# A two-layer decoder trunk: the pooling mixer pipelined, three background advances per pair, and weight low parts made by an adding transfer

## The chip, the cores and the metric

One core of a Trainium2 chip. The metric is the device time of one launch in microseconds, the median over runs. The program is issued in sequence on each engine: TensorE (PE) does matmuls, VectorE (DVE) and ScalarE (ACT) the work on rows, GpSimd (POOL) small things and, here, some transfers, SyncE (SP) issues the loads.

## The reference

Two layers over 1040 tokens (16 meta tokens and 1024 inputs) of width 1024, batch 1, float32:

```
for i in range(DEPTH):                      # 2
    a = rmsnorm(h, norm_mix_pre[i])
    if i % N_MIXERS == 0: m = mla_mixer(a, ...)           # layer 0
    else:                 m = pool_mixer(a, w_group, scale)  # layer 1
    h = h + rmsnorm(m, norm_mix_post[i])
    f = conv_ffn(rmsnorm(h, norm_ffn_pre[i]), w_up, conv_w, conv_b, w_down)
    h = h + rmsnorm(f, norm_ffn_post[i])
```

The pooling mixer works in four groups of 256 channels: the mean over the last 2, 4, 8 or 16 tokens less the token itself, times a 256 x 256 matrix of the group. The MLP has a width-3 causal convolution on both halves of its up-projection (2 x 2816 channels), then silu(gate) times value, then the down-projection.

## The kernel before

All dense work is done with channels on the 128 partitions and tokens along the free axis, in two halves: half 0 has 536 tokens, half 1 504. Every product of two float32 matrices is made of three matmuls per 128 x 128 block: high part by high part, high weight by low activation, low weight by high activation (`mm_half`). A weight tile comes from `wtile`: SP loads 128 x 1024 floats (512 KB) into `wr` (three buffers), ACT casts it to the high part `wh`, DVE subtracts to get the low part `wl` (four buffers each).

The MLP goes layer by layer, half by half, in two parts of 11 channel pairs. `ffn_up` makes for each pair a gate tile and a value tile: 24 matmuls of 506 columns in half 1, 48 of 260 to 268 in half 0 (two column cuts). ACT and DVE evict each into the convolution (`cv`), with a multiplication by `late` first in layer 0, half 0 (`u`). `ffn_down` then sums over the pairs. The PSUM pool has six one-bank buffers in half 1 and three two-bank buffers in half 0, handed out in program order.

Beside that runs the work of the other half, as a generator in the list `bg`: `after_ffn` reads the residual, does the norm behind the MLP (`post`), statistics (`inv_rms_steps`), the pooling mixer (`poolmix`), its norm and the norm ahead of the next MLP. `tick()` takes it one `yield` further, with a higher priority of its instructions in the scheduler; `ffn_up` does that twice per pair, `drain()` takes what is left at the end of a part. The scheduler of the framework then writes one order for each engine, and the engines keep to it. The statistics are a matmul with ones (`ps_st`, L82), a reciprocal root on DVE (`nv` ... `yh`, `yl`, L84 to L70), two diagonal matrices (`diag`, L115, one on DVE, one on POOL) and a matmul that spreads them over the partitions (`ps_bc`, L122).

`poolmix` shapes, for each group g and each of its two channel blocks, `pa` (normed input), g + 1 sums `psm`, `pmx`, and the split `xh` (ACT), `xl` (DVE); then come 24 matmuls of 268 columns in half 0 (12 of 504 in half 1) with the group's weights `pwh`, `pwl`, the eviction `F` on ACT and its sum of squares.

The stages that the text speaks of are named by layer and by the half whose up-projection runs: in "layer 0, half 1" the pooling mixer of half 0 is the background, in "layer 1, half 0" that of half 1.

Of the kernel before, what the change touches and what calls it, by code (L numbers as in the profile page):

```python
# [11 lines left out]
F32 = mybir.dt.float32  # L12
F32R = mybir.dt.float32r
I32 = mybir.dt.int32
ALU = mybir.AluOpType
# [31 lines left out]
class Kern:  # L47
# [553 lines left out]
    def dense(self):  # L601
        tc, nc, io, ctx = self.tc, self.nc, self.io, self.ctx
        P = lambda name, bufs, **kw: ctx.enter_context(tc.tile_pool(name=name, bufs=bufs, reuse_waits="tile", **kw))
        self.wp, self.ab, self.hp, self.gp = P("wp", 4), P("ab", 1), P("hp", 1), P("gp", 1)
        self.fp, self.up, self.tp = P("fp", 8), P("up", 2), P("tp", 5)
        stp = P("stf", 2, space=PSUM)
        self.stps = lambda name: stp.tile([128, 512], F32, tag="st", name=name)
        self.psum = None
        self.banks(1)
        self.dtile = lambda x: self.tp.tile([128, HALF], F32R, tag="x" + x, name="diag", bufs=2)  # L610
        self.H, self.A, self.bg = {}, {}, []

        F, acc = self.wo(0)
        self.bg.append(self.after_mixer(0, F, acc, 0, True))
        F, acc = self.wo(1)
        self.drain()
        self.bg.append(self.after_mixer(1, F, acc, 0, False))
        for L in range(2):
            self.L = L
            for hf in range(2):  # L620
                self.banks(2 - hf)
                Fa = None
                for part in range(2):
                    G = self.ffn_up(hf, part)
                    self.drain()
                    if part == 1 and hf == 0:
                        self.bg.append(self.pre(1, L))
                    if part == 1 and hf == 1 and L == 0:
                        self.bg.append(self.pre(0, 1))
                    if (L, hf, part) == (1, 1, 1):  # L630
                        self.ffn_down_last(part, G, Fa)
                        break
                    F, acc = self.ffn_down(part, G, Fa)
                    Fa = F
                    self.drain()
                else:
                    self.bg.append(self.after_ffn(hf, F, acc, L))
        self.drain()
# [13 lines left out]
    def after_mixer(self, hf, F, acc, L, pre):  # L652
        acc = yield from self.post(hf, F, acc, G_MIXPOST + 8 * L)
        if pre:

            self.late = yield from self.inv_rms_steps(acc, "xh", 2)
            yield from self.pre(hf, L, True)
        else:
            yield from self.ffn_norm(hf, acc)
# [41 lines left out]
        self.O[hf][0].append(hi)  # L701
        self.O[hf][1].append(lo)

    def wtile(self, src, nk, pool=False):
        nc = self.nc
        n = 128 * nk
        r = self.wp.tile([128, 1024], F32, tag="wr", name="wr", bufs=3)
        if pool:
            hi = self.wp.tile([128, 512], F32R, tag="pwh", name="pwh", bufs=1)
            lo = self.wp.tile([128, 512], F32R, tag="pwl", name="pwl", bufs=1)  # L710
        else:
            hi = self.wp.tile([128, 1024], F32R, tag="wh", name="wh")
            lo = self.wp.tile([128, 1024], F32R, tag="wl", name="wl")
        src = src if isinstance(src, list) else [src]
        for i, a in enumerate(src):
            w = n // len(src)
            nc.sync.dma_start(r[:, i * w:i * w + w], a)
        self.split(r[:, :n], hi[:, :n], lo[:, :n], lo_eng="dve")
        return [(hi[:, 128 * k:128 * k + 128], lo[:, 128 * k:128 * k + 128]) for k in range(nk)]

    @staticmethod
# [158 lines left out]
    def ffn_up(self, hf, part):  # L880
# [8 lines left out]
        for jj in range(JH):  # L889
            j = part * JH + jj  # L890
            cv = []
            for gv in range(2):
                idx = gv * NJ + j
                u, = self.mm_half(self.wtile(io["w_up"][L, j, :, gv], KD), ah, al, skip=skip)
                if (L, hf) == (0, 0):
                    t = self.up.tile([128, HALF], F32, tag="u", name="u")
                    nc.vector.tensor_tensor(t, u, self.late, op=ALU.mult)
                    u = t
                p0 = G_CONV + (L * 2 * NJ + idx) * 4
                c = self.tp.tile([128, HALF], F32, tag="t", name="cv")[:, :n]  # L900
                nc.scalar.activation(c, u[:, pad:pad + n], AF.Identity, bias=self.par(p0 + 3), scale=self.par(p0 + 2))  # L901
                for x in (1, 0):

                    o = max(0, 2 - x - pad)
                    nc.vector.scalar_tensor_tensor(c[:, o:], u[:, pad + x - 2 + o:pad + x - 2 + n], self.par(p0 + x),  # L905
                                                   c[:, o:], op0=ALU.mult, op1=ALU.add)
                cv.append(c)
                if gv == 0:
                    nc.scalar.activation(c, c, AF.Silu)  # L909
                    self.tick()  # L910
            nc.vector.tensor_tensor(cv[0], cv[0], cv[1], op=ALU.mult)  # L911
            hi = self.gp.tile([128, HALF], F32R, tag=f"gh{jj}", name="gh")[:, :n]
            lo = self.gp.tile([128, HALF], F32R, tag=f"gl{jj}", name="gl")[:, :n]
            self.split(cv[0], hi, lo, lo_eng="dve")
            gh.append(hi)
            gl.append(lo)
            self.tick()
# [57 lines left out]
    def poolmix(self, hf, R):  # L975
        nc, io = self.nc, self.io
        F, acc = [], None
        n_tok = HALVES[hf][1]
        end = n_tok + 16
        for g in range(4):  # L980
            win = 2 << g
            xh, xl = [], []
            for kk in range(2):
                k = 2 * g + kk
                a = self.tp.tile([128, HALF + 16], F32, tag="tc", name="pa")[:, :end]
                if hf == 0:
                    nc.gpsimd.memset(a[:, :16], 0.0)
                else:
                    nc.gpsimd.tensor_scalar(a[:, :16], self.phalo[:, k], 1.0, 0.0, op0=ALU.mult, op1=ALU.add)
                nc.vector.scalar_tensor_tensor(a[:, 16:], self.H[hf][k], self.par(G_MIXPRE + 8 + k), R,  # L990
                                               op0=ALU.mult, op1=ALU.mult)
                if hf == 0:
                    nc.gpsimd.tensor_scalar(self.phalo[:, k], a[:, n_tok:end], 1.0, 0.0,
                                            op0=ALU.mult, op1=ALU.add)
                s = a
                for l in range(g + 1):
                    d = 1 << l
                    lo, hi = 2 * d - 1, end
                    n = self.tp.tile([128, HALF + 16], F32, tag="tc", name="psm")[:, :end]
                    nc.vector.tensor_tensor(n[:, lo:hi], s[:, lo:hi], s[:, lo - d:hi - d], op=ALU.add)  # L1000
                    s = n
                mx = self.tp.tile([128, HALF + 16], F32, tag="tc", name="pmx")[:, :end]
                nc.vector.scalar_tensor_tensor(mx[:, 16:], s[:, 16:], 1.0 / win, a[:, 16:],
                                               op0=ALU.mult, op1=ALU.subtract)
                if hf == 0:
                    nc.vector.tensor_tensor(mx[:, 16:32], s[:, 16:32], self.par(G_CNT + 16 * g, 16), op=ALU.mult)
                    nc.vector.tensor_tensor(mx[:, 16:32], mx[:, 16:32], a[:, 16:32], op=ALU.subtract)
                hi_ = self.tp.tile([128, HALF], F32R, tag="xh", name="xh", bufs=2)[:, :n_tok]
                lo_ = self.tp.tile([128, HALF], F32R, tag="xl", name="xl", bufs=2)[:, :n_tok]
                self.split(mx[:, 16:], hi_, lo_, lo_eng="dve")  # L1010
                xh.append(hi_)
                xl.append(lo_)
                if kk == 0:
                    W = self.wtile(io["w_pool"][g], 4, True)
                yield
            for m in range(2):
                ps = self.mm_half([W[2 * kk + m] for kk in range(2)], xh, xl)
                f = self.fp.tile([128, HALF], F32, tag="F", name="F")[:, :n_tok]
                self.evac(f, ps, self.par(G_PS + 2 * g + m))
                F.append(f)  # L1020
                acc = self.addsq(acc, f)
            yield
        return F, acc


# [50 lines left out]
```

## Time and profile before

| | |
|---|---|
| median of 3 runs | 2246.76 us (2246.19 to 2248.37) |
| profiled run, its own time | 2246.28 us |
| its span | 2244.5 us |
| mean granted clock of PE | 0.984 of full speed |
| PE busy | 2154.0 us, 96% |
| DVE busy | 1459.2 us, 65% |
| ACT busy | 1046.9 us, 47% |
| POOL busy | 415.1 us, 18% |

The profiled run's time is 1.8 us longer than its span, which counts from the first instruction to the last. A row of the timeline gives the start, the length and the instruction, in brackets the idle time of its engine ahead of it and what ended that.

### The profile page before, as it was taken

The numbers are of one execution on the slowest core, as the hardware profiler recorded it, in microseconds if no ns is written. First come the engines' busy times: TensorE is split into PE (matmuls) and PEld (weight loads), VectorE is DVE, ScalarE is ACT, GpSimd is POOL, SyncE is SP. The second block draws the span as 40 slices with busy tenths as digits, with TensorE's granted clock in tenths as the row PEclk, the third lists the DMA queues.
The fourth block names the chain that finished last, engine by engine and source line by source line (L and its number), as shares of the span: only waits on it lengthen the run. The fifth ranks groups of instructions, "written<-read, shape, count | busy, mean of one in ns | idle before, by whom it ended". The sixth has DMA issues, their size and how long they took to land.

```text
span 2244.5 us, 36441 instructions
## 1 busy us (share of the span) xinstructions
PE 2154.0 (96%) x13968; PEld 1966.9 (88%) x13968; DVE 1459.2 (65%) x2686; ACT 1046.9 (47%) x1934; POOL 415.1 (18%) x755
## 2 busy tenths in 40 slices
PE   8889999998999999999998999999899999999996
PEld 8788888887989999999886888899899998888886
DVE  7877777776488725665887555587745557634655
ACT  6367777776454423433553344344433433433431
POOL 5677676764000000000000000000000000000001
PEclk9999999998999999999999999999999999999998
DMA  5011111114343232233223322422242245233321
GB/s 163 22 36 31 30 34 31 25 55 134 114 161 122 82 98 95 89 93 121 93 72 100 128 98 86 130 77 86 86 129 94 68 132 178 86 86 111 99 89 46
DMA packets 82902, 202.76 MB, mean 90 GB/s; under 512 B 10548, under 2 KB 31668, under 8 KB 82728
## 3 DMA queue, kind: packets, MB, share of 16 engines
q1 hardware_dynamic: 82584, 200.18, 28.5%
q8 instruction: 110, 1.80, 0.3%
q14 instruction: 64, 0.52, 0.1%
q10 hardware_dynamic: 144, 0.25, 0.0%
HBM read 179.15 MB, written 16.97 MB: 87 GB/s over the span
## 4 chain that ended last, share of the span: by engine, by line
PE 87%; DVE 5%; ACT 3%; issue 2%; POOL 2%; DMA 1%; SPq 0%; DVEq 0%; ACTq 0%; POOLq 0%
PE ps_m L758 72%; PE ps_t L579 2%; PE ps_s L528 2%; PE ps_o L564 1%; PE ps_o L565 1%; PE ps_s L530 1%; PE ps_s L529 1%; ACT P L542 1%; DVE ps_s L537 1%; PE ps_qk L409 1%; PE ps_st L82 1%; PE ps_qk L411 1%; PE ps_qk L410 1%; PE ps_bc L122 1%; DVE F L826 1%
## 5 line engine op out<-in xcount | busy, mean ns | idle before, releaser
L70 DVE TENSOR_TENSOR wl<-wr,wh 128x1024 fp32r<-128x1024 f32 (+3 forms) x316 | 349.4, 1106 | 420.2 <-ACT wh L64 411.8
L64 ACT CAST wh<-wr 128x1024 fp32r<-128x1024 f32 (+3 forms) x316 | 301.2, 953 | 591.9 <-PE ps_m L758 526.0
L758 PE MATMUL ps_m<-ah,wh 128*128 128x506 f32 (+2 forms) x2112 | 564.1, 321 | 3.4 <-ACT cv L901 1.7
L758 PE MATMUL ps_m<-al,wh 128*128 128x506 f32 (+2 forms) x2112 | 566.7, 322 | 0.0
L758 PE MATMUL ps_m<-ah,wl 128*128 128x506 f32 (+2 forms) x2112 | 563.3, 321 | 0.0
L758 PEld LDWEIGHTS ps_m<-ah,wh 128*128 128x128 f32 x2112 | 353.1, 189 | 34.9 <-ACT cv L901 1.9
L758 PEld LDWEIGHTS ps_m<-al,wh 128*128 128x128 f32 x2112 | 353.0, 189 | 28.3 <-issue 0.7
L758 PEld LDWEIGHTS ps_m<-ah,wl 128*128 128x128 f32 x2112 | 353.1, 189 | 27.8 <-issue 0.5
L758 PE MATMUL ps_m<-gh,wh 128*128 128x268 f32 (+3 forms) x1088 | 288.8, 318 | 1.9 <-ACT F L767 1.9
L758 PE MATMUL ps_m<-gh,wl 128*128 128x268 f32 (+3 forms) x1088 | 287.7, 317 | 0.0
L758 PE MATMUL ps_m<-gl,wh 128*128 128x268 f32 (+3 forms) x1088 | 287.4, 317 | 0.0
L905 DVE SCALAR_TENSOR_TENSOR cv<-ps_m,params,cv 128x504 f32<-128x504 f32 (+1 forms) x264 | 196.0, 744 | 3.2
L758 PEld LDWEIGHTS ps_m<-gh,wh 128*128 128x128 f32 x1088 | 182.9, 189 | 16.1 <-ACT F L767 2.1
L758 PEld LDWEIGHTS ps_m<-gh,wl 128*128 128x128 f32 x1088 | 181.9, 189 | 14.1 <-issue 0.5
L758 PEld LDWEIGHTS ps_m<-gl,wh 128*128 128x128 f32 x1088 | 182.2, 189 | 13.1
L115 POOL TENSOR_TENSOR diag<-ident,yl 65x260 fp32r<-65x260 f32 (+5 forms) x27 | 33.4, 1237 | 716.0 <-DVE yl L70 675.9
L64 ACT CAST gh<-cv 128x504 fp32r<-128x504 f32 (+2 forms) x88 | 54.7, 622 | 168.8 <-DVE cv L911 168.8
L542 ACT ACTIVATE P<-ps_s,stat 116x116 f32<-116x116 f32 (+9 forms) x160 | 111.5, 699 | 32.7 <-DVE stat L537 25.1
L579 PE MATMUL ps_t<-ident,P 116*116 116x116 f32 x720 | 113.2, 266 | 10.1 <-DVE ptl L593 5.4
L547 POOL TENSOR_SCALAR P<-P,stat 116x116 f32<-116x116 f32 (+2 forms) x144 | 109.3, 760 | 54.1 <-DVE stat L545 47.8
L909 ACT ACTIVATE cv<-cv 128x504 f32<-128x504 f32 (+2 forms) x88 | 55.8, 634 | 134.9 <-DVE cv L905 134.9
L579 PEld LDWEIGHTS ps_t<-ident,P 116*116 116x116 f32 x720 | 83.4, 136 | 23.3 <-DVE ptl L593 5.5
(199 smaller groups left out, 3600.1 us busy)
## 6 DMA issues: line engine op xcount, KB each, us to landing
wr<-in_w_up SPq DMA_DIRECT2D x176, 512.0 KB, 3.5
wr<-in_w_down SPq DMA_DIRECT2D x56, 384.0 KB, 3.1
wr<-in_w_down SPq DMA_DIRECT2D x56, 320.0 KB, 2.9
wr<-in_w_o SPq DMA_DIRECT2D x16, 512.0 KB, 3.8
resid<-H SPq DMA_DIRECT2D x16, 268.0 KB, 4.2
H<-resid SPq DMA_DIRECT2D x16, 268.0 KB, 3.4
xt<-in_x SPq DMA_DIRECT2D x32, 130.0 KB, 2.3
resid<-H SPq DMA_DIRECT2D x16, 252.0 KB, 3.7
```

The costliest lines, as they stand in the source:

```text
L64: nc.scalar.copy(hi, src)
L70: eng.tensor_tensor(lo, src, hi.bitcast(F32), op=ALU.subtract)
L82: nc.tensor.matmul(ps[:w, i:i + 1], acc[:, w * i:w * i + w], self.ones, start=True, stop=True)
L115: eng.tensor_tensor(t, self.ident[:w, :w].unsqueeze(1).broadcast_to([w, n, w]), part.bitcast(F32).unsqueeze(2).broadcast_to([w, n, w]), op ...
L122: nc.tensor.matmul(pb[:, :g * w], self.ones_r[:w], t[:, q:q + g].rearrange("p n w -> p (n w)"), start=i == 0, stop=i == 1)
L528: nc.tensor.matmul(ps[:n, x, :w], qh[:, qs], kh[:, ks], start=True, stop=False)
L542: nc.scalar.activation(dst, ps, AF.Exp, bias=mx[:n, 1:2], scale=-1.0, accum_out=es[:n, gi:gi + 1])
L547: nc.gpsimd.tensor_scalar(P[:n, :nk], P[:n, :nk], rs[:n], 1.0, op0=ALU.mult, op1=ALU.mult)
L579: nc.tensor.transpose(pt[:kn, x * QT:x * QT + n], Pi[:n, k0:k0 + kn], self.ident[:n, :n])
L758: nc.tensor.matmul(p, w, x[k][:, skip + c0:skip + c0 + m], start=k == 0 and w is wh and x is xh, stop=k == last and w is wl)
L905: nc.vector.scalar_tensor_tensor(c[:, o:], u[:, pad + x - 2 + o:pad + x - 2 + n], self.par(p0 + x), c[:, o:], op0=ALU.mult, op1=ALU.add)
L909: nc.scalar.activation(c, c, AF.Silu)
```

## The change

It has four parts. The up-projection's value tile is split into two runs of matmuls with a third `tick` between them, so a pair takes three advances in place of two. In `poolmix` the shaping of group g + 1 stands ahead of the matmuls of group g, and there are 9 yields in place of 12. In the first part of layer 0, half 1, and of layer 1, half 0 (44 weight tiles), the low part is no longer a subtraction on DVE: ACT writes the negative of the high part into `wl`, and a transfer of POOL's queue adds the 512 KB of `wr` onto it. Some temporaries get three buffers in place of two, and `u` shares the ring of `xl`.

```diff
-    def wtile(self, src, nk, pool=False):
+    def wtile(self, src, nk, pool=False, add=False):
...
-        self.split(r[:, :n], hi[:, :n], lo[:, :n], lo_eng="dve")
+        if add:
+
+            nc.scalar.copy(hi[:, :n], r[:, :n])
+            nc.scalar.activation(lo[:, :n], r[:, :n], AF.Copy, scale=-1.0)
+            nc.gpsimd.dma_start(lo[:, :n].bitcast(F32), r[:, :n], accum_op=ALU.add)
+        else:
+            self.split(r[:, :n], hi[:, :n], lo[:, :n], lo_eng="dve")
...
-                u, = self.mm_half(self.wtile(io["w_up"][L, j, :, gv], KD), ah, al, skip=skip)
+
+                W = self.wtile(io["w_up"][L, j, :, gv], KD, add=part == 0 and hf != L)
+                ps = self.mm_half(W[:KD // 2], ah, al, 0, KD, skip=skip, n=n + pad)
+                if gv == 1:
+                    self.tick()
+                u, = self.mm_half(W[KD // 2:], ah, al, KD // 2, KD, ps, skip, n + pad)
                 if (L, hf) == (0, 0):
-                    t = self.up.tile([128, HALF], F32, tag="u", name="u")
+                    t = self.tp.tile([128, HALF], F32, tag="xl", name="u", bufs=3)
...
+        X = [([], []) for _ in range(4)]
+        W = None
+        for g in range(5):
             for kk in range(2):
...
+                if g < 4:
+                    for dst, t in zip(X[g], shape(g, kk)):
+                        dst.append(t)
+                    yield
+                if g and kk == 0:
+                    for m in range(2):
+                        ps = self.mm_half([W[2 * x + m] for x in range(2)], *X[g - 1])
+                        f = self.fp.tile([128, HALF], F32, tag="F", name="F")[:, :n_tok]
+                        self.evac(f, ps, self.par(G_PS + 2 * (g - 1) + m))
+                        F.append(f)
+                        acc = self.addsq(acc, f)
+                if g < 4 and kk == 0:
                     W = self.wtile(io["w_pool"][g], 4, True)
-                yield
...
+        yield
         return F, acc
```

`shape` is the body of the old inner loop, unchanged but for three buffers of `xh` and `xl`. (`wl` is of the type fp32r, so the negative copy is rounded like `wh`, and the sum is again `wr` less `wh`.)

The order that results is shown at three places. First PE in layer 0, half 0, between two up-projection tiles (`ah`, `al` the activation, `wh`, `wl` the weights), at the second statistics of the other half. Before:

```order
L758 MATMUL ps_m<-ah,wh 128x268 x2
L758 MATMUL ps_m<-al,wh 128x268 x2
L82 MATMUL ps_st<-ones,acc 63x1 x8
L758 MATMUL ps_m<-ah,wl 128x268 x2
L758 MATMUL ps_m<-ah,wh 128x268 x2
```

The broadcast `ps_bc<-diag,ones_r` stood 74 rows behind this `ps_st`. Now the same engine has there:

```order
L764 MATMUL ps_m<-ah,wh 128x268 x2
L764 MATMUL ps_m<-al,wh 128x268 x2
L764 MATMUL ps_m<-ah,wl 128x268 x2
L82 MATMUL ps_st<-ones,acc 63x1 x8
L122 MATMUL ps_bc<-diag,ones_r 128x504 x2
L764 MATMUL ps_m<-ah,wh 128x268 x2
L764 MATMUL ps_m<-al,wh 128x268 x2
```

The broadcast has moved up to the ones matmul, with nothing between them.

Second PE in layer 0, half 1, at the end of the matmuls of group 2 of the pooling mixer and the first four of group 3 (`xh`, `xl` its input, `pwh`, `pwl` its weights). Before, with the down-projection's first tile (`gh`, `gl`) behind:

```order
L758 MATMUL ps_m<-xh,pwh 128x268 x4
L758 MATMUL ps_m<-xl,pwh 128x268 x2
L758 MATMUL ps_m<-xh,pwl 128x268 x2
L758 MATMUL ps_m<-xl,pwh 128x268 x2
L758 MATMUL ps_m<-xh,pwl 128x268 x2
L758 MATMUL ps_m<-xh,pwh 128x268 x4
L758 MATMUL ps_m<-gh,wh 128x504
```

Now the same rows stand between two tiles of the up-projection, with two more blocks of the first five rows ahead of them (the second half of group 1 and the first half of group 2):

```order
L764 MATMUL ps_m<-xh,pwh 128x268 x4
L764 MATMUL ps_m<-xl,pwh 128x268 x2
L764 MATMUL ps_m<-xh,pwl 128x268 x2
L764 MATMUL ps_m<-xl,pwh 128x268 x2
L764 MATMUL ps_m<-xh,pwl 128x268 x2
L764 MATMUL ps_m<-xh,pwh 128x268 x4
L764 MATMUL ps_m<-ah,wh 128x506
L764 MATMUL ps_m<-al,wh 128x506
```

So 12 + 24 + 4 pool matmuls have moved between two neighbouring tiles of the up-projection. DVE has, from the conv rows of the tile ahead (`cv_14627`) to the `pmx` that these last four need, 20 full-width instructions and 4 of 16 columns; the last twelve are:

```order
L1014 SCALAR_TENSOR_TENSOR pmx_14464<-psm_14462,pa_14454 128x536
L1001 SCALAR_TENSOR_TENSOR pa_14509<-H_13709,params_70,R_14110 128x536
L1017 TENSOR_TENSOR pmx_14464<-psm_14462,params_70 128x16
L1011 TENSOR_TENSOR psm_14513<-pa_14509 128x551
L1018 TENSOR_TENSOR pmx_14464<-pmx_14464,pa_14454 128x16
L1011 TENSOR_TENSOR psm_14515<-psm_14513 128x549
L70 TENSOR_TENSOR xl_14469<-pmx_14464,xh_14468 128x536
L1011 TENSOR_TENSOR psm_14517<-psm_14515 128x545
L1011 TENSOR_TENSOR psm_14519<-psm_14517 128x537
L1014 SCALAR_TENSOR_TENSOR pmx_14521<-psm_14519,pa_14509 128x536
L1017 TENSOR_TENSOR pmx_14521<-psm_14519,params_70 128x16
L1018 TENSOR_TENSOR pmx_14521<-pmx_14521,pa_14509 128x16
```

The shaping of group 3's first block (`pa_14509` to `pmx_14521`) has moved in among that of group 2, behind the conv of the tile ahead.

Third ACT in layer 1, half 0, ahead of the cast of group 3's first input. Before:

```order
L769 ACTIVATE F_18399<-ps_m_18392,params_70 128x504
L780 ACTIVATE sq_18389<-F_18387 128x504
L909 ACTIVATE cv_18375<-cv_18375 128x520
L780 ACTIVATE sq_18401<-F_18399 128x504
L64 CAST wh_18784<-wr_18783 128x640
L901 ACTIVATE cv_18459<-ps_m_18410,params_70 128x520
L64 CAST xh_18481<-pmx_18479 128x504
```

Now:

```order
L775 ACTIVATE F_17984<-ps_m_17977,params_70 128x504
L720 CAST wh_18301<-wr_18300 128x1024
L721 ACTIVATE wl_18302<-wr_18300 128x1024
L786 ACTIVATE sq_17974<-F_17972 128x504
L786 ACTIVATE sq_17986<-F_17984 128x504
L64 CAST xh_17929<-pmx_17927 128x504
```

A weight tile's cast and its new copy have moved between the eviction and the cast; the up-projection's own eviction (`cv_18459` before, `cv_18036` now) has moved ahead of these rows.

## Rows read from the trace of the kernel before

**Rows 1.** The page's first part: busy us, share of the span, instructions.

```profile
PE 2154.0 (96%) x13968; PEld 1966.9 (88%) x13968; DVE 1459.2 (65%) x2686; ACT 1046.9 (47%) x1934; POOL 415.1 (18%) x755
```

**Rows 2.** Waits of PE, 1000 to 1320 us: us in total, times, longest.

```profile
PE ps_m L758 <- ACT xh L64: 12.4, 2, 10.1
```

**Rows 3.** Waits of PE, 1420 to 1700 us.

```profile
PE ps_m L758 <- ACT xh L64: 2.7, 1, 2.7
PE ps_m L758 <- ACT F L767: 1.9, 1, 1.9
PE ps_m L758 <- ACT cv L901: 1.7, 1, 1.7
PE ps_m L758 <- DVE xl L70: 1.1, 1, 1.1
PE ps_m L758 <- ACT F L769: 0.3, 1, 0.3
```

**Rows 4.** Timeline of PE around the two waits of layer 0, half 1.

```profile
1169.72 1.06 PE L758 MATMUL ps_m<-xh,pwh 128*128 128x268 f32 x4 [2.30 <-ACT xh L64]
...
1173.72 0.40 PE L758 MATMUL ps_m<-ah,wl 128*128 128x506 f32 x1
1173.95 0.39 PE L758 MATMUL ps_m<-ah,wh 128*128 128x506 f32 x1
...
1190.18 1.26 PE L758 MATMUL ps_m<-xh,pwh 128*128 128x268 f32 x4 [10.12 <-ACT xh L64]
```

**Rows 5.** Windows: length, busy PE, PEld, DVE, ACT, POOL, granted clock, DMA share, GB/s.

```profile
1169.70:1173.50 3.80, 3.78 (x12) 3.19 (x13) 3.77 (x7) 0.63 (x1) 0.00 (x0) 0.55 0.35 108
1590.00:1600.00 10.00, 10.00 (x65) 9.51 (x64) 6.13 (x10) 4.25 (x7) 0.00 (x0) 0.84 0.06 8
```

**Rows 6.** Windows over layer 0, half 0 (first) and half 1, in up-projection.

```profile
673.30:729.40 56.10, 56.10 (x455) 55.17 (x454) 50.08 (x79) 25.89 (x36) 3.79 (x1) 1.00 0.37 122
1050.00:1177.40 127.40, 125.10 (x577) 104.15 (x578) 108.19 (x182) 61.60 (x94) 5.72 (x15) 0.99 0.27 85
```

**Rows 7.** Timeline of ACT and DVE ahead of the 10.12 us wait.

```profile
1178.03 0.77 ACT L901 ACTIVATE cv<-ps_m,params 128x504 f32<-128x504 f32 x1
1178.90 1.52 DVE L905 SCALAR_TENSOR_TENSOR cv<-ps_m,params,cv 128x504 f32<-128x504 f32 x2
...
1189.30 0.16 DVE L1007 TENSOR_TENSOR pmx<-pmx,pa 128x16 f32<-128x16 f32 x1
1189.49 0.64 ACT L64 CAST xh<-pmx 128x536 fp32r<-128x536 f32 x1 [6.29 <-DVE pmx L1007]
```

**Rows 8.** Timeline of statistics: POOL in layer 0, half 0, then a whole chain.

```profile
678.62 3.79 POOL L115 TENSOR_TENSOR diag<-ident,yl 63x504 fp32r<-63x504 f32 x1 [21.59 <-DVE yl L70]
...
1206.62 1.08 PE L82 MATMUL ps_st<-ones,acc 128*67 128x1 f32 x16
1208.32 0.15 DVE L84 TENSOR_SCALAR nv<-ps_st 67x8 f32<-67x8 f32 x1
...
1211.00 1.42 POOL L115 TENSOR_TENSOR diag<-ident,yl 67x536 fp32r<-67x536 f32 x1 [22.20 <-DVE yl L70]
```

**Rows 9.** Groups by shape: busy, mean ns of one, idle before and releasers.

```profile
L70 DVE TENSOR_TENSOR wl<-wr,wh 128x1024 fp32r<-128x1024 f32 x196 | 240.5, 1227 | 267.9 <-ACT wh L64 263.0 <-PE ps_m L758 2.3
L64 ACT CAST wh<-wr 128x1024 fp32r<-128x1024 f32 x196 | 206.1, 1051 | 334.8 <-PE ps_m L758 289.0 <-issue 40.2 <-DMA wr<-in_w_o 5.2
```

**Rows 10.** DMA issues: count, KB each, median us to landing.

```profile
wr<-in_w_up SPq DMA_DIRECT2D x176, 512.0 KB, 3.5
...
wr<-in_w_dqkv SPq DMA_DIRECT2D x6, 336.0 KB, 5.2
```

**Rows 11.** Timeline of POOL, two copies of 16 columns in layer 1, half 0.

```profile
1477.70 0.20 POOL L989 TENSOR_SCALAR pa<-phalo 128x16 f32<-128x16 f32 x1 [25.09 <-DVE acc L781]
1564.00 2.06 POOL L989 TENSOR_SCALAR pa<-phalo 128x16 f32<-128x16 f32 x1 [15.98 <-DVE psm L1000]
```

More of the change, by code (lines that the diff above doesn't have):

```diff
@@ L604, in dense @@
         self.wp, self.ab, self.hp, self.gp = P("wp", 4), P("ab", 1), P("hp", 1), P("gp", 1)
-        self.fp, self.up, self.tp = P("fp", 8), P("up", 2), P("tp", 5)
+        self.fp, self.tp = P("fp", 8), P("tp", 5)
         stp = P("stf", 2, space=PSUM)
@@ L609, in dense @@
         self.banks(1)
-        self.dtile = lambda x: self.tp.tile([128, HALF], F32R, tag="x" + x, name="diag", bufs=2)
+        self.dtile = lambda x: self.tp.tile([128, HALF], F32R, tag="x" + x, name="diag", bufs=3)
         self.H, self.A, self.bg = {}, {}, []
@@ L654, in after_mixer @@
         if pre:
-            self.late = yield from self.inv_rms_steps(acc, "xh", 2)
+            self.late = yield from self.inv_rms_steps(acc, "xh", 3)
             yield from self.pre(hf, L, True)
@@ L979, in poolmix, with shape @@
         end = n_tok + 16
-        for g in range(4):
+        def shape(g, kk):
             win = 2 << g
-            xh, xl = [], []
-            for kk in range(2):
[L984 to L1013, printed above, removed]
-                    W = self.wtile(io["w_pool"][g], 4, True)
-                yield
[L1016 to L1022, printed above, removed]
@@ new lines, in shape @@
+            k = 2 * g + kk
+            a = self.tp.tile([128, HALF + 16], F32, tag="tc", name="pa")[:, :end]
+            if hf == 0:
+                nc.gpsimd.memset(a[:, :16], 0.0)
+            else:
+                nc.gpsimd.tensor_scalar(a[:, :16], self.phalo[:, k], 1.0, 0.0, op0=ALU.mult, op1=ALU.add)
+            nc.vector.scalar_tensor_tensor(a[:, 16:], self.H[hf][k], self.par(G_MIXPRE + 8 + k), R,
+                                           op0=ALU.mult, op1=ALU.mult)
+            if hf == 0:
+                nc.gpsimd.tensor_scalar(self.phalo[:, k], a[:, n_tok:end], 1.0, 0.0,
+                                        op0=ALU.mult, op1=ALU.add)
@@ new lines, in shape @@
+            s = a
+            for l in range(g + 1):
+                d = 1 << l
+                lo, hi = 2 * d - 1, end
+                n = self.tp.tile([128, HALF + 16], F32, tag="tc", name="psm")[:, :end]
+                nc.vector.tensor_tensor(n[:, lo:hi], s[:, lo:hi], s[:, lo - d:hi - d], op=ALU.add)
+                s = n
+            mx = self.tp.tile([128, HALF + 16], F32, tag="tc", name="pmx")[:, :end]
+            nc.vector.scalar_tensor_tensor(mx[:, 16:], s[:, 16:], 1.0 / win, a[:, 16:],
+                                           op0=ALU.mult, op1=ALU.subtract)
@@ new lines, in shape @@
+            if hf == 0:
+                nc.vector.tensor_tensor(mx[:, 16:32], s[:, 16:32], self.par(G_CNT + 16 * g, 16), op=ALU.mult)
+                nc.vector.tensor_tensor(mx[:, 16:32], mx[:, 16:32], a[:, 16:32], op=ALU.subtract)
+            hi_ = self.tp.tile([128, HALF], F32R, tag="xh", name="xh", bufs=3)[:, :n_tok]
+            lo_ = self.tp.tile([128, HALF], F32R, tag="xl", name="xl", bufs=3)[:, :n_tok]
+            self.split(mx[:, 16:], hi_, lo_, lo_eng="dve")
+            return hi_, lo_
```

## The prediction, made before the changed kernel had run

> **What bounds the kernel now.** I read the page first, then the waits of TensorE (PE) in the two stages in which the pooling mixer runs as background work, then windows and the timeline around the waits found. The page shows PE busy 96% of the span, VectorE (DVE) 65%, ScalarE (ACT) 47%, GpSimd (POOL) 18% [rows 1]. PE's work is not changed by the edit: the order has as many matmuls after as before. So only PE's idle time can move, and it lies in few places. In layer 0, half 1, PE waits 12.4 us in two events, both for the cast `xh` of the pooling mixer on ACT [rows 2]; in layer 1, half 0, it waits five times, 7.7 us together [rows 3]. The timeline shows the two events: 2.30 and 10.12 us, each ahead of the four matmuls that read a first `xh` [rows 4].
>
> A wait costs more than its length. In the 3.80 us behind the 2.30 us wait the mean granted clock is 0.55, so it ran nearly all of it at the lower of the two levels (half of 2.4 GHz): 3.80 x 0.45 = 1.7 us lost. The stretch around the last wait of layer 1 stands at 0.84 over 10 us: 1.6 us lost [rows 5]. The bill of before is then 12.4 + 2 x 1.7 = 15.8 us in layer 0, half 1, and 7.7 + 1.6 = 9.3 us in layer 1, half 0. The stage of layer 0, half 0, has no bill: in its 56 us PE is busy all of the time [rows 6].
>
> Why PE waits: the second event's cast came when `pmx` was done, and DVE had worked without a gap since its conv rows at 1178.90: 15 full-width instructions and 2 narrow ones to 1189.46, so (10.56 - 0.33) / 15 = 0.68 us for a full-width one [rows 7]. DVE works its order in sequence. PE starves where the schedule puts pool matmuls closer behind a tile than DVE can shape their input.
>
> **The change part by part.**
>
> *Three advances per pair, layer 0, half 0.* Before, the ones matmul of the statistics (`ps_st`) and the broadcast (`ps_bc`) had 74 rows of up-projection between them; now nothing stands between (first place of the order above). PE has to sit through the whole chain: ones to `nv` 1208.32 - 1207.70 = 0.6 us, `nv` to the end of POOL's `diag` 1212.42 - 1208.32 = 4.1 us, 4.7 us together [rows 8]. POOL's `diag` of this very stage and shape took 3.79 us beside a busy DVE against 1.42 in that chain [rows 8], so the upper bound is 7.1 us. Below, some of it could be covered by matmuls still in flight: 4 us, with no loss of clock. I take 4.7 and a fall of the clock, 1.7, less 0.4 for matmuls in flight: **+6 us**. It is nearer the low end since the two DVE instructions that follow the chain there are few. What is late next are three evictions `u`, which stand behind `diag` on DVE; they start before POOL is done and are hidden by it. The same pair of rows in the other stages keeps a distance of 30 or more rows.
>
> *Pool matmuls of layer 0, half 1.* With three advances, two advances of one pair bring the matmuls of groups 1, 2 and the first four of group 3 between the same two tiles: 12 + 24 + 4 matmuls (second place of the order). At 0.123 us for 268 columns (56.10 / 455) [rows 6], the 36 ahead of group 3's are 4.4 us of work. DVE has, from the conv rows of the tile ahead to the `pmx` of group 3, 20 full-width instructions and 4 narrow: 20 x 0.68 + 4 x 0.17 = 14.3 us; an eviction on ACT ahead of them (0.8) and the cast behind (0.64) [rows 7] with some 0.2 between make 16.0. PE waits 16.0 - 4.4 = 11.6, and 1.7 of clock. The first group costs as well: its cast stands behind the tile's own eviction on ACT, and DVE has 9 full-width and 2 narrow instructions, 6.5 us, to do from the second last tile's end plus 1 us of eviction and 0.8 of cast, where a tile of 24 matmuls takes 24 x 0.23 = 5.5 us [rows 4]: 2.8 us, and 1.7. Four weight copies on ACT (4 x 1.05 [rows 9]) now stand ahead of group 2's second cast; up to 3 us of them could come on top, I take half. Sum 11.6 + 1.7 + 2.8 + 1.7 + 1.5 = 19.3 against 15.8: **+3.5 us** (bounds 0 and +8). The pipelined order doesn't remove this wait, it moves it from the start of the down-projection into the up-projection.
>
> *Layer 1, half 0.* Here ACT is late. Between the eviction `F` of group 2 and the cast `xh` of group 3 now stand a cast and the new copy of a weight tile, and two squares (third place of the order): 2 x 1.05 + 4 x 0.64 = 4.7 us with the eviction and the cast themselves [rows 7, 9], about 5 with latencies, and 1.6 of clock. The waits like those of before that stay, for evictions of the post step and first casts, I put at 3.9, half of the 7.7 of now [rows 3]. 5.0 + 1.6 + 3.9 = 10.5, and up to 1.5 where ACT waits for a load whose slot is still being added from, taken at half: 11.3 against 9.3: **+2 us** (bounds -2 and +6).
>
> *Fourth stage (layer 1, half 1).* Its background work has no statistics and no pool; 33 advances in place of 22 only bring it earlier. Nothing; the six PSUM buffers of that half cover it.
>
> *Low parts by adding transfers.* DVE loses 44 subtractions of 1.227 us, 54 us; ACT gains 44 copies like its casts of 1.05, 46 us [rows 9]. ACT was busy 61.6 of 127.4 us in the stage, DVE 108.2 [rows 6]: neither becomes the bound by its sum. PE lost 2.3 us in those 127 us, so the relief of DVE has almost nothing to win there. New is the transfer, X us long, between the copy and PE. It is hidden if a slot of `wr` turns round in three tiles, 3 x 5.5 = 16.5 us: load 3.5 [rows 10], two ACT passes 2.1, about 2 of queueing, which leaves X up to 8.9. The trace has no adding transfer. Bounds: below, the load of the same size, 3.5 us; above, the slowest load, 336 KB in 5.2 us, scaled to 512 KB: 7.9 [rows 10]. I take 7, twice the plain load, since the target is read too. It stays below 8.9, and the sum gets nothing from it. The Trainium skill (DMA: Bandwidth & Descriptors, section on the anatomy of a GpSimd-path DMA) gives 2.0 us plus bytes over 436 GB/s; for 512 KB that is an estimate of 3.2 us for a plain copy, by which the sum stays the same.
>
> Queued behind the adds on POOL stand the halo copies, memsets and `diag`, for which DVE, and for `diag` PE, waits. POOL idled 25 us ahead of one such copy [rows 11], which covers an add's wait of some us; without that cover each us is a us of PE.
>
> *Buffers.* `u`, `xh`, `xl` and the diagonals go from two to three buffers: less waiting or none, nothing counted. The same number of loads goes through SP, with W of a group one step later, behind its shape.
>
> *Sum.* 6 + 3.5 + 2 = +11.5 us on the profiled run's own 2246.28: 2257.8. That run lies 0.5 us below the median of the three, so I say **2258 us**.
>
> **The rivals.**
>
> *Faster: the pool waits vanish.* If DVE, 54 us lighter, runs ahead far enough that every first `xh` is there when PE comes to it, 15.8 + 9.3 are won and 6 lost: 2246.3 - 25.1 + 6 = 2227 us. For it speaks DVE's 85% in that stage (108.19 / 127.40) [rows 6]. Against it: the long row of shaping stands behind the conv of the tile ahead, which needs that tile's end, and the subtractions removed aren't in it. It decides where at most 6 of the 20 full-width rows are left when that tile ends. 12%.
>
> *The change does nothing that shows.* The long waits come out as before, and the statistics' gap is half covered: 2243 to 2250. For it: two of my three terms are differences of like numbers. 18%.
>
> *The add becomes the bound.* If X is above 8.9, the slot's ring is the clock: each us above it costs 1/3 us in each of 44 tiles, 15 us. X = 10 gives 2258 + 16 = 2274, X = 12 gives 2304. For it: a 16-column copy on POOL took 2.06 us in the midst of DVE work and 0.20 elsewhere [rows 11], so what POOL does for a transfer may take ten times as long while DVE runs, and DVE hardly pauses. Against it: 1.9 us more on 7 is at the limit, not over it. 12%. The Trainium skill (SBUF — State Buffer, section "Who interferes with whom") says that a DMA seen stalled by DVE is one issued from GpSimd, whose descriptors wait for a port pair that DVE holds; it infers that two-input DVE instructions spare the descriptors. The 2.06 us row agrees that POOL is held up; whether descriptors are, no row here shows.
>
> **How the numbers follow.** The forecast has 58%, on 2250 to 2270 by its bounds (+4, 0, -2 to +9, +8, +6, not all at one end). 2244 to 2276 leaves out the faster rival (12%) and the larger part of the slow add (8%). A measurement of this kernel tells 0.2%, 4.5 us, from no change. Faster 0.13, same 0.19, slower 0.68.
>
> **What would show it.** Right: a PE wait of 4 to 7 us at the broadcast in layer 0, half 0, for `diag`; one of about 11 us for ACT's `xh` of group 3 in layer 0, half 1, now ahead of an `ah` tile; one of about 5 us for `xh` in layer 1, half 0, with ACT busy; adds of 3.5 to 8 us and no PE waits for `wl`. Wrong: PE waits for `wl` in every tile (slow add), a broadcast without a gap, or group 3's `xh` ready when PE arrives.

## The result and the profile after

The changed kernel takes 2285.4 us (median of 5 runs, 2281.74 to 2289.98) against 2248.37 (2246.19 to 2248.99): 1.0172 times as long, 95% interval 1.0161 to 1.0182. The forecast was 2258, in 2244 to 2276. The direction was right, the size was not: 37 us slower in place of about 11. The profiled run took 2289.87 us. The first part of its page:

```profile
PE 2171.7 (95%) x13968; PEld 1982.4 (87%) x13968; DVE 1410.0 (62%) x2642; ACT 1086.9 (48%) x1978; POOL 454.1 (20%) x799
```

Beside [rows 1] PE has as many matmuls and is busy 17.7 us longer (its mean granted clock is 0.973 of full speed against 0.984), DVE lost 49 us, ACT gained 40. No engine but PE is near its limit. Where the time went shows in windows over the three stages that differ: layer 0, half 0; layer 0, half 1 with its first down-projection; layer 1, half 0 with its first down-projection. Columns as in [rows 5]; first the kernel before (two stages), then the changed one:

```profile
1042.70:1258.60 215.90, 203.48 (x971) 169.78 (x970) 166.71 (x290) 95.99 (x151) 9.49 (x20) 0.97 0.31 98
1440.20:1664.00 223.80, 216.11 (x1706) 209.04 (x1705) 160.21 (x265) 94.66 (x139) 10.30 (x12) 0.99 0.30 95
```

```profile
645.30:789.20 143.90, 139.73 (x1112) 137.57 (x1113) 111.30 (x188) 60.47 (x82) 4.12 (x3) 0.98 0.34 107
1050.10:1288.30 238.20, 209.56 (x971) 174.16 (x970) 145.46 (x271) 113.62 (x171) 30.05 (x39) 0.92 0.53 136
1470.80:1706.40 235.60, 222.05 (x1704) 214.50 (x1705) 138.62 (x245) 111.51 (x158) 25.09 (x31) 0.96 0.53 137
```

Layer 0, half 0 had 137.1 us up to its first down-projection (the same boundaries in the timeline, its first `ah` matmul to its first `gh`): +6.8. Layer 0, half 1: +22.3, of which PE's idle time is 16.2 (238.20 - 209.56 against 215.90 - 203.48) and 6.1 the clock (0.92 against 0.97). Layer 1, half 0: +11.8. That is 40.9 of the 43.6 us between the two spans. The waits of PE in the first, the second and the third stage, as in [rows 2] and [rows 3]:

```profile
PE ps_bc L122 <- DVE diag L115: 4.0, 1, 4.0
```

```profile
PE ps_m L764 <- ACT xh L64: 24.5, 4, 10.4
PE ps_bc L122 <- DVE diag L115: 3.9, 1, 3.9
```

```profile
PE ps_m L764 <- ACT xh L64: 8.6, 2, 7.7
PE ps_m L764 <- ACT F L775: 2.8, 1, 2.8
PE ps_st L82 <- DVE acc L787: 1.2, 1, 1.2
```

PE still waits for the first `xh` of a mixer group. But now ACT, which casts it, waits for something that the kernel before did not have in this stage. ACT's longest group of waits from 1050 to 1288 us:

```profile
ACT wh L720 <- DMA wr<-in_w_up: 30.9, 9, 6.3
```

ACT stands at the cast of a weight tile because its load has not come. The adding transfer is short: 5.1 us in the median, as the DMA issues show, beside the load's 3.6.

```profile
wr<-in_w_up SPq DMA_DIRECT2D x176, 512.0 KB, 3.6
wl<-wr POOLq DMA_DIRECT2D x44, 512.0 KB, 5.1
```

So look at when loads are issued. Timelines of PE at its longest wait, and of SP, POOL and ACT ahead of it:

```profile
1129.88 1.26 PE L764 MATMUL ps_m<-xh,pwh 128*128 128x268 f32 x4 [10.35 <-ACT xh L64]
```

```profile
1083.36 0.33 SPq L717 DMA_DIRECT2D wr<-in_w_pool  x1
1089.59 0.33 SPq L717 DMA_DIRECT2D wr<-in_w_up  x1
1090.01 0.38 SPq L717 DMA_DIRECT2D wr<-in_w_pool  x1
1097.90 0.33 SPq L717 DMA_DIRECT2D wr<-in_w_up  x1
1103.92 0.33 SPq L717 DMA_DIRECT2D wr<-in_w_pool  x1
1112.41 0.33 SPq L717 DMA_DIRECT2D wr<-in_w_up  x1
1122.92 0.33 SPq L717 DMA_DIRECT2D wr<-in_w_up  x1
```

```profile
1107.85 0.86 POOL L722 DMA_DIRECT2D wl<-wr  x1 [10.11 <-PE ps_m L764]
...
1118.31 0.87 POOL L722 DMA_DIRECT2D wl<-wr  x1 [5.04 <-ACT wl L721]
```

```profile
1116.00 1.05 ACT L720 CAST wh<-wr 128x1024 fp32r<-128x1024 f32 x1 [5.80 <-DMA wr<-in_w_up]
1116.95 1.06 ACT L721 ACTIVATE wl<-wr 128x1024 fp32r<-128x1024 f32 x1
1117.92 0.61 ACT L920 ACTIVATE cv<-cv 128x504 f32<-128x504 f32 x1
1118.43 0.76 ACT L912 ACTIVATE cv<-ps_m,params 128x504 f32<-128x504 f32 x1
```

Every second load is one of the mixer's weights (`in_w_pool`), in the same three buffers `wr`. Such a tile keeps its place until its cast `pwh` may be written, and that single buffer is free only when PE is done with the group before. The mixer's loads issued at 1090.01 and 1103.92 are cast only here:

```profile
1139.08 0.62 ACT L64 CAST pwh<-wr 128x512 fp32r<-128x512 f32 x1
1158.87 0.62 ACT L64 CAST pwh<-wr 128x512 fp32r<-128x512 f32 x1
```

So from 1103.92 to 1139 at least two of the three places are held, and the up-projection has one at most. Its loads come at 1112.41 and 1122.92, 10.5 us apart, one turn of that place: the add issued at 1107.85 lets the load go at 1112.41, the cast runs at 1116.00, the copy at 1116.95, the next add at 1118.31, the next load at 1122.92. A tile of matmuls lasts 5.5 us. Behind the cast, ACT has the conv evictions, which free PSUM and feed DVE, and the cast `xh` itself. So the load of 1122.92 leads straight to PE's longest wait: ACT waits for it, and the `xh` that PE needs at 1129.88 stands three instructions behind it.

```profile
1126.63 1.04 ACT L720 CAST wh<-wr 128x1024 fp32r<-128x1024 f32 x1 [3.98 <-DMA wr<-in_w_up]
...
1129.20 0.63 ACT L64 CAST xh<-pmx 128x536 fp32r<-128x536 f32 x1
```

### The profile page after: what moved, and what is told of

The parts are those of the page before. It is cut to its first block, busy times and chain, and to the rows that moved or that the text cites. A ratio compares the mean times of both kernels' runs of the same rounds, so it can differ in the third digit from the quotient of the medians.

```text
span 2288.1 us, 36519 instructions
## 1 busy us (share of the span) xinstructions
PE 2171.7 (95%) x13968; PEld 1982.4 (87%) x13968; DVE 1410.0 (62%) x2642; ACT 1086.9 (48%) x1978; POOL 454.1 (20%) x799
## 4 chain that ended last, share of the span: by engine, by line
PE 82%; DMA 5%; DVE 5%; ACT 4%; issue 2%; POOL 2%; SPq 0%; DVEq 0%; ACTq 0%; POOLq 0%
PE ps_m L764 69%; PE ps_t L579 2%; DMA wl<-wr 2%; PE ps_s L528 2%; DMA wr<-in_w_up 2%; PE ps_o L564 1%; PE ps_o L565 1%; PE ps_s L529 1%; PE ps_s L530 1%; ACT P L542 1%; DVE ps_s L537 1%; PE ps_qk L409 1%; PE ps_qk L410 1%; PE ps_qk L411 1%; PE ps_st L82 1%
## 5 line engine op out<-in xcount | busy, mean ns | idle before, releaser
L764 PE MATMUL ps_m<-ah,wh 128*128 128x506 f32 (+2 forms) x2112 | 570.7, 324 | 6.0 <-ACT F L775 2.8
L764 PE MATMUL ps_m<-al,wh 128*128 128x506 f32 (+2 forms) x2112 | 573.2, 325 | 0.0
L70 DVE TENSOR_TENSOR wl<-wr,wh 128x1024 fp32r<-128x1024 f32 (+3 forms) x272 | 294.8, 1084 | 416.8 <-ACT wh L64 413.6
L64 ACT CAST wh<-wr 128x1024 fp32r<-128x1024 f32 (+3 forms) x272 | 254.9, 937 | 508.4 <-PE ps_m L764 450.5
L764 PEld LDWEIGHTS ps_m<-ah,wh 128*128 128x128 f32 x2112 | 358.2, 192 | 39.1 <-issue 3.6
L764 PEld LDWEIGHTS ps_m<-al,wh 128*128 128x128 f32 x2112 | 358.0, 192 | 28.3 <-issue 0.7
L722 POOL DMA_DIRECT2D wl<-wr x44 | 38.3, 870 | 472.7 <-ACT wl L721 456.3
```

Source lines behind the costliest of these rows:

```text
L64: nc.scalar.copy(hi, src)
L70: eng.tensor_tensor(lo, src, hi.bitcast(F32), op=ALU.subtract)
L722: nc.gpsimd.dma_start(lo[:, :n].bitcast(F32), r[:, :n], accum_op=ALU.add)
L764: nc.tensor.matmul(p, w, x[k][:, skip + c0:skip + c0 + m], start=k == 0 and w is wh and x is xh, stop=k == last and w is wl)
```

## The experiments

Two theories stood against each other. The **ring theory**: the add makes a place of `wr` busy longer, and the mixer's weights take too many places, so loads are late. The **shaping theory**, which is the prediction's own: DVE's shaping stands too close behind a tile, and the add is innocent. All kernels are made from the changed one or from the one before. "Advances" are those per pair; "piped" is the pipelined mixer with the new buffers; the last word of a row says whose ring the mixer's weights load into. The stages' lengths (us) are from the timeline of each, from the first matmul of a stage to that of the next. Each ratio was measured beside runs of the kernel before on the same chip (medians 2247.15 to 2248.60).

| kernel | advances, mixer, low parts, mixer weights in | median us | ratio to before, 95% | L0 half 0 | L0 half 1 | L1 half 0 |
|---|---|---|---|---|---|---|
| before | 2, old, subtract, wr | 2248.37 | 1 | 137.1 | 215.9 | 223.8 |
| after | 3, piped, add, wr | 2285.4 | 1.0161 to 1.0182 | 143.9 | 238.2 | 235.6 |
| no_add | 3, piped, subtract, wr | 2270.49 | 1.0087 to 1.0117 | 142.8 | 230.7 | 226.5 |
| add_only | 2, old, add, wr | 2244.37 | 0.9976 to 0.9994 | 137.1 | 211.4 | 225.0 |
| own_ring_t4 | 3, piped, add, own | 2258.18 | 1.0036 to 1.0066 | 143.4 | 220.4 | 222.5 |
| two_ticks | 2, piped, add, wr | 2250.29 | 1.0001 to 1.0021 | 137.0 | 211.3 | 235.1 |
| t4_alone | 3, piped, add, wr | 2281.87 | 1.0134 to 1.0164 | 144.3 | 232.6 | 231.4 |
| own_ring_no_add | 3, piped, subtract, own | 2270.44 | 1.0081 to 1.0111 | 143.4 | 227.2 | 226.7 |
| third_only | 3, old, subtract, wr | 2279.07 | 1.0119 to 1.0153 | 137.1 | 241.5 | 229.9 |
| two_ticks_own_ring | 2, piped, add, own | 2230.13 | 0.9904 to 0.9935 | 137.0 | 199.5 | 223.4 |
| add_own_ring | 2, old, add, own | 2244.45 | 0.9979 to 0.9997 | 137.1 | 208.5 | 226.6 |
| two_ticks_own_no_add | 2, piped, subtract, own | 2245.32 | 0.9980 to 0.9999 | 137.0 | 209.4 | 224.4 |
| third_bufs | 3, old, subtract, wr, new buffers | 2284.28 | 1.0150 to 1.0180 | 143.0 | 240.4 | 229.3 |
| pipe_only | 2, piped, subtract, wr | 2241.11 | 0.9965 to 0.9983 | 137.0 | 208.5 | 224.4 |

**no_add**: the add undone.

```diff
-                W = self.wtile(io["w_up"][L, j, :, gv], KD, add=part == 0 and hf != L)
+                W = self.wtile(io["w_up"][L, j, :, gv], KD)
```

> The changed kernel with the subtraction on VectorE back; third advance, pipelined mixer and buffers stay. Ring theory (the three wr buffers turn round too slowly, because an add holds each some 6 us longer while the mixer's weights take every second place of the ring): layer 0, half 1 falls from 238 to about 219 us (up- and first down-projection), layer 1, half 0 from 236 to about 226, the kernel to about 2257; ScalarE's waits for wr loads under 1 us each. Shaping theory (the prediction's: VectorE's shaping of the mixer stands too close behind a tile, the add is innocent): VectorE gets 54 us more work, so both stages stay as long or get longer, 2285 or more. Both: the gap of 4 us at the broadcast in layer 0, half 0 stays.

Between the two: 15 us faster with 54 us more work on DVE, so the add is not innocent; but layer 0, half 1 is 230.7, not 219. A second cause is in it. Nor do ACT's waits for loads of the up-projection fall under 1 us each there: five are left, 10.2 us together.

**add_only**: the add on the kernel before, the same lines of `wtile` as in the change.

> The kernel before with the adding transfer alone, in the same 44 tiles; two advances and the mixer as before, whose weights take every fourth place of the ring. Ring theory: the add is dear only together with the denser mixer weights, so little shows here: 2247 to 2256. If the add's own delay between the load and the matmul is the cost, whatever the ring holds: 20 us or more, 2265 to 2280. Shaping theory: VectorE is relieved, 2240 to 2247.

Some 3.5 us faster than before. With the mixer's weights in every fourth place the add costs nothing and its relief shows, which is what the shaping theory had expected; the ring theory had put no gain here. The third guess, that the add's delay costs by itself, is out.

**own_ring_t4**: a buffer for the mixer's weights alone, the conv ring cut from five to four to make room.

```diff
-        r = self.wp.tile([128, 1024], F32, tag="wr", name="wr", bufs=3)
         if pool:
+            r = self.wp.tile([128, 512], F32, tag="pwr", name="pwr", bufs=1)
+        else:
+            r = self.wp.tile([128, 1024], F32, tag="wr", name="wr", bufs=3)
+        if pool:
...
-                c = self.tp.tile([128, HALF], F32, tag="t", name="cv")[:, :n]
+                c = self.tp.tile([128, HALF], F32, tag="t", name="cv", bufs=4)[:, :n]
```

> The changed kernel with a buffer of its own for the mixer's weight load (one, 512 columns), so wr serves the up-projection alone; the ring of the conv tiles cv is cut from 5 to 4 buffers to make room. Ring theory: an add may then take up to 8.9 us and takes 5.1, so ScalarE's waits for loads go and the kernel falls to about 2258 to 2265 (the prediction's own sum and its waits for shaping stay). Shaping theory: nothing changes but for the conv ring, 2283 to 2290.

2258.18, 27 us less. ACT's waits for loads in layer 0, half 1 fall from 30.9 us in nine to 3.7 in one, PE's from 28.7 to 14.7:

```profile
ACT wh L723 <- DMA wr<-in_w_up: 3.7, 1, 3.7
```

```profile
PE ps_m L767 <- ACT xh L64: 11.9, 3, 6.4
PE ps_m L767 <- ACT pwh L64: 2.8, 1, 2.8
```

**t4_alone**: its control, the second hunk above without the first.

> Control for the own ring: the changed kernel with the conv ring cv at 4 buffers and nothing else. If the 27 us that the own buffer won came from the wr ring: no gain here, 2280 to 2295. If the shorter conv ring did it (another order of the engines): 2255 to 2265.

2281.87: of the 27 us, some 24 are those of the place in `wr` (22 by the ratios), the rest is the conv ring's, no more than the spread of the runs.

**two_ticks**: the third advance undone, the split into two runs of matmuls kept.

```diff
-                if gv == 1:
-                    self.tick()
```

> The changed kernel without the third advance per pair; pipelined mixer, adding transfer and buffers stay. Both theories: the gap at the broadcast in layer 0, half 0 goes, 7 us. Ring theory: the mixer's weights take every third place or so, half of the ring's loss is left: 2262 to 2270. Shaping theory: the clusters of the mixer's matmuls are taken apart, both stages come back to their old length, 2245 to 2255.

2250.29, 35 us less. Layer 0, half 1 falls to 211.3, as the shaping theory said; layer 1, half 0 stays at 235.1, as it did not say. In this trace two of the up-projection's loads stand between two of the mixer's.

**own_ring_no_add**: own_ring_t4 with the edit of no_add.

> The own buffer for the mixer's weights (conv ring 4) with VectorE's subtraction back in place of the add; third advance and pipelined mixer stay. Ring theory: with wr for the up-projection alone the add costs nothing and its relief of VectorE is worth what it was on the kernel before, some 4 us: 2259 to 2266. If the add still delays weights there: faster than 2255.

2270.44, slower than expected by either: with three advances the relief by the add is worth 12 us, not 4. Beside no_add (2270.49) it shows that the own buffer, with the other order that it brings, is worth nothing without the add. Ring and add hurt together only.

**third_only**: the third advance put into the kernel before.

```diff
-                u, = self.mm_half(self.wtile(io["w_up"][L, j, :, gv], KD), ah, al, skip=skip)
+                W = self.wtile(io["w_up"][L, j, :, gv], KD)
+                ps = self.mm_half(W[:KD // 2], ah, al, 0, KD, skip=skip, n=n + pad)
+                if gv == 1:
+                    self.tick()
+                u, = self.mm_half(W[KD // 2:], ah, al, KD // 2, KD, ps, skip, n + pad)
```

> The kernel before with the third advance alone (the value tile's matmuls in two runs, a tick between); old mixer, VectorE's subtraction, old buffers. Mixer weights take every third place of the ring here. Ring theory: without the add a place is free some 6 us sooner, so waits for wr loads stay small; 7 us for the broadcast in layer 0, half 0, and shaping waits like those of before: 2252 to 2260. Shaping theory: three advances cluster the mixer by themselves and that is most of the change's cost: 2265 to 2285.

2279.07, as the shaping theory had it: three advances alone cost 30 us. PE waits 6.6 us for `diag` at the broadcast of layer 0, half 1, ahead of the mixer. The waits over the mixer's stretch there (from the first `pa` on DVE to its last matmul, 1109.31 to 1192.23) show the rest:

```profile
PE ps_m L758 <- ACT xh L64: 25.1, 4, 7.5
DVE acc L781 <- ACT sq L780: 12.0, 2, 6.1
DVE pwl L70 <- ACT pwh L64: 7.7, 1, 7.7
...
ACT F L769 <- PE ps_m L758: 21.2, 4, 6.3
ACT xh L64 <- DVE pmx L1011: 15.2, 7, 4.1
```

PE waits for ACT, ACT for DVE and for PE, DVE for ACT. No engine is full: the group goes round in sequence, shaping, cast, matmuls, eviction `F`, square, sum `acc`, and the next group's shaping stands behind that sum in DVE's order. Windows over the same stretch, of the kernel before, of third_only and of two_ticks_own_ring (below):

```profile
1116.61:1199.21 82.60, 70.18 (x335) 59.36 (x334) 67.85 (x110) 38.14 (x64) 3.55 (x15) 0.92 0.21 64
```

```profile
1109.31:1192.23 82.92, 58.33 (x260) 49.14 (x261) 55.20 (x92) 29.02 (x49) 2.75 (x15) 0.82 0.17 53
```

```profile
1104.91:1186.59 81.68, 81.68 (x402) 69.38 (x401) 65.90 (x112) 49.54 (x77) 14.77 (x24) 1.00 0.61 147
```

The mixer takes 82 to 83 us in all three. What changes is how much of the up-projection the schedule has put beside it: 335 matmul records, 260, 402. In this stage the third advance takes three tiles of cover away from the old mixer, and the mixer does not get shorter for it. That its length stays is not general, though. With the pipelined mixer the third advance does shorten the stretch, as the windows of pipe_only (two advances, below) and no_add (three) show:

```profile
1114.42:1189.82 75.40, 69.72 (x336) 58.86 (x335) 66.15 (x110) 36.59 (x61) 5.93 (x15) 0.95 0.24 76
```

```profile
1116.41:1177.36 60.95, 43.25 (x196) 36.73 (x197) 49.54 (x84) 24.56 (x43) 9.34 (x15) 0.75 0.19 61
```

The stretch loses 14 us, but the matmuls beside it fall from 336 to 196, and PE's idle time (length less busy time) grows by 12 us in both pairs: 12.4 to 24.6 in the old mixer, 5.7 to 17.7 in the pipelined one. The clock adds to it, 0.95 to 0.75. In layer 1, half 0, the old mixer's stretch falls from 95.9 to 72.2 us and PE's idle time in it still grows, from 4.1 to 9.1.

**two_ticks_own_ring**: the edits of two_ticks and own_ring_t4 together.

> Two advances, pipelined mixer, adding transfer, own buffer for the mixer's weights (conv ring 4). Ring theory: with two advances layer 1, half 0 still took 235 us, with mixer weights in every third place; with the own buffer it falls to 222 to 225, layer 0, half 1 stays at 209 to 212: 2236 to 2241, faster than the kernel before. Shaping theory: the stage of layer 1 is long by its shaping, so it stays: 2248 to 2252.

2230.13, faster than both kernels (0.9904 to 0.9935 of before) and than expected. Layer 0, half 1 has no PE wait left; its window:

```profile
1044.10:1243.60 199.50, 199.50 (x970) 167.11 (x969) 143.63 (x262) 112.73 (x170) 29.54 (x39) 1.00 0.63 160
```

**add_own_ring**: add_only with the edit of own_ring_t4.

> The kernel before with the adding transfer and the own buffer for the mixer's weights (conv ring 4); two advances, old mixer. If pipelining the mixer is a part of what made the best kernel so far (2230): the old mixer's long wait for group 3 stays, 2240 to 2246. If the add and the free ring do it alone: 2227 to 2233.

2244.45: the old mixer's wait for group 3 stays (6.84 us in the timeline). The pipelining is a needed part of 2230.

**two_ticks_own_no_add**: two_ticks_own_ring with the edit of no_add.

> The best kernel so far (two advances, pipelined mixer, own buffer) with VectorE's subtraction back in place of the add. If VectorE's load in the mixer's stretch is what sets the waits, its 54 us come back as waits in part: 2238 to 2246. If with two advances the pipelining alone removes the waits: 2228 to 2233.

2245.32: so is the add, worth 15 us there. (Against pipe_only, 2241.11, below, the own buffer without the add is 4 us slower.)

**third_bufs**: third_only with the new buffers (three of `xh`, `xl` and `diag`, `u` in the ring of `xl`).

> The kernel before with the third advance and the changed buffers (three of xh, xl and diag, u in the ring of xl); old mixer, subtraction. The third advance alone left layer 0, half 0 at 137 us, so if the buffers together with it bring broadcast and ones matmul together, the 4 us gap appears and the stage takes 143 to 144 us. If the pipelined mixer is needed for it: 137. The kernel: 2270 to 2288 in either case, less where the third buffer of xh and xl helps the mixer.

The gap at the broadcast appears in layer 0, half 0, 143.0 us against 137.1 in third_only. The waits of PE there:

```profile
PE ps_bc L122 <- DVE diag L115: 4.0, 1, 4.0
```

It needs the third advance and the buffers, not the pipelined mixer; two_ticks, with the buffers and two advances, has none.

**pipe_only**: the changed kernel with the edits of two_ticks and no_add.

> Pipelined mixer and changed buffers alone: two advances, subtraction, mixer weights in the ring of wr. Load theory (VectorE's work per pair sets the waits, the ring is harmless without the add): the long waits for group 2 and 3 of the old mixer spread and shrink, 2238 to 2247. Shaping theory as predicted (pipelining only moves the waits): 2245 to 2252. If dense mixer weights hurt without the add too: 2255 or more.

2241.11, 6 us faster than before in its own comparison: with two advances the pipelined mixer takes the 12.4 us of waits of layer 0, half 1 down to 5.7.

With these runs five pairs differ by the third advance alone: before to third_only (+30 us), pipe_only to no_add (+29), two_ticks to the changed kernel (+35), two_ticks_own_ring to own_ring_t4 (+28), two_ticks_own_no_add to own_ring_no_add (+25). Whatever stands beside it, it is the largest single cost of the change.

## Why the prediction was right and wrong

**Two steps failed.** In the prediction's own terms the miss splits in two. Everything but the add is no_add: 2270.49, +22 us where the sum had +11.5. The add on top costs 15 more, where the sum had nothing.

**The add** was priced at nothing by the step "It is hidden if a slot of `wr` turns round in three tiles, 3 x 5.5 = 16.5 us". The add's own time was in its bounds (5.1 us measured, 7 taken, 8.9 allowed). But the ring's three places do not serve three tiles. The prediction said that W of a group goes through SP "one step later" and did not ask whose place it takes: the mixer's weights stand in the same ring, in every fourth place before, in every second or third after, and each waits there for the group ahead, so that for a time one place of three is left. own_ring_t4 against t4_alone puts the step at 24 us, and its mechanism is shown by ACT's waits for loads, which go with it. The rival "The add becomes the bound" named the right resource and the wrong condition: X above 8.9 was not needed, fewer places were. The 15 us are this loss (27 with the conv ring) less a relief of DVE that the sum had at nothing too: 12 us, own_ring_no_add to own_ring_t4.

**The pool matmuls of layer 0, half 1,** were priced at +3.5 (bounds 0 and +8). Without the add, in no_add, that stage stands at +14.8 against before, of which PE's idle time is 9.5 and the clock the rest; the other two stand at +5.7 (predicted +6) and +2.6 (+2). The failed part is the wait itself: 11.6 us were put at group 3, where PE waits 2.2, and only 2.8 and a share of copies elsewhere.

**That own_ring_t4 takes 2258.18, the forecast's 2258, is luck.** It is the changed kernel without the ring's loss, and its stages stand at +6.3 (predicted +6), +4.5 (+3.5) and -1.3 (+2) against before. But behind these sums stand larger terms that cancel: the third advance costs 28 us there, and the pipelined mixer, the add's relief and the own buffer give 18 back (2230.13 against 2248.60).

**Layer 0, half 0: right in size, incomplete in cause.** PE waited 4.0 us for `diag` (4.7 predicted), and the stage grew by 6.8, with the clock. I put it down to the third advance alone; third_only has no such gap, third_bufs has it.

**Layer 0, half 1: the wait moved, as said, but the bookkeeping hid the parts.** The changed kernel has PE waits at first `xh` rows, one of 10.4 us, but ahead of the first group and not of group 3, and four in place of two. The +3.5 was a difference of stalls at single places. The runs show three larger terms in it: the third advance costs 25.6 us in this stage on the kernel before (third_only), the pipelining gives 7.4 (pipe_only), and the add up to 9.9 where the ring is free (two_ticks_own_no_add to two_ticks_own_ring). That DVE's relief "has almost nothing to win there" was wrong: I read it from the 127 us ahead of the mixer's end, where PE lost 2.3 us, and not from the mixer's stretch in the new order. The gap of 3.9 us at the broadcast in this stage was not foreseen either: there are over 30 rows of PE between it and the ones matmul, but DVE's chain stands behind a conv that waited 8.12 us for ACT, which had itself waited 6.30 for a load. Without the add the gap is there too (3.2 us in no_add, 6.6 in third_only), with two advances it is 0.2 us at most. The timeline of DVE:

```profile
1106.64 1.52 DVE L916 SCALAR_TENSOR_TENSOR cv<-ps_m,params,cv 128x504 f32<-128x504 f32 x2 [8.12 <-ACT cv L912]
1108.08 0.15 DVE L84 TENSOR_SCALAR nv<-ps_st 67x8 f32<-67x8 f32 x1
```

**Layer 1, half 0: too small for the same reason.** +11.8 in place of +2; +2.6 without the add, -1.3 with it and the mixer's own buffer. A wait of about 5 us for `xh` was foreseen, behind an eviction, a weight tile's two passes and two squares on ACT. It came there with 7.7 us, and the surplus is again the ring's: in the midst of that row ACT waits for a load.

```profile
1582.40 1.04 ACT L720 CAST wh<-wr 128x1024 fp32r<-128x1024 f32 x1 [2.77 <-DMA wr<-in_w_up]
```

**POOL's queue.** What spoke for a slow add, that DVE starves what POOL does for transfers, did not come: the add takes 4.5 us at least and 7.8 at most over the 44, and its issue holds POOL 0.85 to 1.04 us, with DVE busy 61% of layer 0, half 1 (145.46 / 238.20). The Trainium skill (SBUF — State Buffer, "Who interferes with whom") infers that two-input DVE instructions spare the descriptors; these times agree with that. By the Trainium skill's fit for a plain copy on POOL's path (DMA: Bandwidth & Descriptors, the section on that path's anatomy) the estimate was 3.2 us; the adding transfer measured 5.1.

## What to carry to other kernels

Before counting a longer step as hidden behind a ring of buffers, list who else allocates from that ring, in the new order, and how long each keeps its place; a tile that waits for a consumer far down the program takes a place away from the stream. Advancing background work faster need not pay: where its steps wait for one another, it shortens the background less than it takes away the foreground work that covers it (here 75 to 61 us, against 336 to 196 matmuls), and the difference is idle time. A total that comes out as forecast does not confirm its terms; compare them one by one. Test the parts of a bundled change by themselves: here two advances, the pipelined mixer, the add and an own buffer make 0.992 of the time before, while the third advance and the shared ring turned the same ideas into 1.017.

## What the runs showed of the hardware

An adding transfer of 512 KB within SBUF landed 5.1 us after its issue in the median (4.5 to 7.8), against 3.6 for a plain load of the same size, and POOL was held 0.87 us by each issue. In the other kernels with the add the median was 4.9 to 5.8. The adds also slowed the loads beside them. In layer 0, half 1, up to its down-projection, a load of the up-projection landed 3.5 us after its issue in the median before and 3.2 to 3.4 in the other kernels without the add looked at (no_add, pipe_only, two_ticks_own_no_add), against 3.9 in the changed kernel and 4.7 in the fastest, two_ticks_own_ring, where the adds took 4.9 and 6.1; the DMA share of the whole stage rose from 0.31 to 0.53 and 0.63. Over all 176 loads of a launch the median hides this, 3.5 against 3.6.
